# Down projection of a gated MLP: 36 of 43 input tiles in seven block products for eight

## The chip, the cores and the metric

The kernel runs on one core of one Trainium2 chip. The metric is the device time of one execution in microseconds. Three runs of the kernel before took 2181.3, 2181.68 and 2183.76 us; their median is 2181.68 us. The core has TensorE (matmuls, PE in the rows; PEld is its weight load, which overlaps), VectorE (DVE), ScalarE (ACT), GpSimd (POOL) and SyncE (SP). In this kernel SP issues nearly all loads and POOL the writes to memory and the accumulating loads.

## The reference, cut to what matters

One layer of a hybrid block on 512 tokens of width 2048 with a prefix of 256 context tokens. What the change touches is the gated MLP at the end:

```python
FFN_DIM = ((8 * D_MODEL // 3 + 127) // 128) * 128      # 5504 = 43 tiles of 128

def conv_ffn(h, w_up, cw, cb, w_down):
    u = dwconv3(h @ w_up, cw, cb)
    a, g = jnp.split(u, 2, axis=-1)
    return (a * jax.nn.silu(g)) @ w_down

mod_l = (jax.nn.silu(c) @ w_ada[l] + b_ada[l])[:, None, :]
sh_a, sc_a, gt_a, sh_f, sc_f, gt_f = jnp.split(mod_l, 6, axis=-1)
...
hf_l = modulate(rms_norm(x, g_ffn_norm[l]), sh_f, sc_f)
x = x + gt_f * conv_ffn(hf_l, w_up[l], ffn_conv_w[l], ffn_conv_b[l], w_down[l])
return rms_norm(x, g_final)
```

All data are float32. The gate `gt_f` (the last 16 of the 96 column tiles of `w_ada`) is needed only where the down projection ends.

## The kernel before

Activations lie transposed: a tile is 128 features by 512 tokens. Every float32 operand of a large product is split into a rounded part and the rest (`hilo`, `split`, `split4`: a cast on ScalarE, then a subtraction on VectorE), and `mm3` (L170 to L174) makes three matmuls of it: high by high, high by low, low by high. `late_both` works off the column tiles of `w_ada` beside other work: each tile is 1 MB, in two halves, and each half is one VectorE product-and-sum of 128 x 1024 (L240). Column tiles 32 to 79 are done before the up projection and 80 to 95 in the first group of the down projection.

The out projection (`whole`, L889) makes one output tile of 128 features at a time from one row of weights, in four splits of 512 columns. Its last two output tiles are made in two halves of the tokens, so that the norm after it can begin.

The up projection (loop over `f`, from L1129) makes one input tile of the down projection per turn, its gate and its value together. It takes input tiles, tokens and these two outputs in pairs, and makes seven block products of 256 columns (`product`) in place of eight. Two of the weight sums come from loads that add into a tile already loaded (`up_load`, issued by POOL), two from VectorE (L1144, L1145). Two of the seven products of a tile (`finish`) are made in the next turn. `acts` does convolution, gate and product, and writes the tile to memory (`y_d`, L990).

The down projection walks over three groups of output tiles, `DG` = 6, 6 and 4, one PSUM bank per output tile. Within a group it goes through all 43 input tiles: a load of weights, a load of the tile `y`, a split of both, and `n` times `mm3` on 512 columns. Loads are issued three input tiles ahead. In the last group the last eight input tiles are held on chip and done for the first half of the tokens, then for the second, so that the final norm of the first half runs beside the second. `down_end` (L1193) multiplies by the gate and adds the residual.

The order of the instructions on each engine is made by a planner, which works through the program by priority and by its own costs; each engine then works in that order. `keep` holds chosen instructions in the order of the program. Background generators (`bg`, advanced by `pump`) put small steps between products. The ring `t2` has 58 buffers of 128 x 512. In the up projection 56 of them hold its operands.

Of the kernel before, what the change touches and what calls it, by code (L numbers as in the profile page):

```python
# [17 lines left out]
P = 128  # L18
# [22 lines left out]
DG = [(0, 6), (6, 6), (12, 4)]  # L41

LAST = 8
# [3 lines left out]
NORM_AT = [(0, 3), (0, 7), (1, 7)]  # L47
# [15 lines left out]
def block_kernel(ctx, tc, xt, ctxt, ctxn, c, c_ctx, w_ada, small, w_in, w_inc, w_q, w_kv, w_out,  # L63
                 w_out_first, w_up, w_up_first, w_dn0, w_dn1, w_dn2, consts, out):
# [17 lines left out]
    y_d = dr.tile([NF, P, T], F32, name="y_d")  # L82
# [150 lines left out]
    late = {"t": 32, "raw": None, "end": 80}  # L233
# [655 lines left out]
    def whole(raw, xs, nm, ps=None, cols=slice(0, T), ld=None):  # L889
# [55 lines left out]
    for m in range(NK - 2):  # L945
        x_tile(m)
        residual(m, pss[m] if m < G else whole([load(w_out[m - G], D, f"o{m}r")], mix, f"o{m}", ld=ada_spare))
# [5 lines left out]
    for h in range(2):  # L953
        for i in range(2):
            residual(NK - 2 + i, whole(raws[i], mix, f"o{NK - 2 + i}{h}", pso[i], HS[h]), HS[h])
# [4 lines left out]
    assert late["t"] == 80 and late["raw"] is None  # L960
    SP.dma_start(sv_d, sv)
    ph1.close()
    rw = ctx.enter_context(tc.tile_pool(name="rw", bufs=1, side="right", reuse_waits="tile"))
    cp = ctx.enter_context(tc.tile_pool(name="cp", bufs=1, side="right", reuse_waits="tile"))
# [19 lines left out]
    def acts(f, g, a):  # L984
# [5 lines left out]
        G_.dma_start(y_d[f], ua)  # L990
# [122 lines left out]
    down_order = deque((g, k) for g in range(len(DG)) for k in range(NF))  # L1113

    def down_fetch():
        if down_order:
            g, k = down_order.popleft()
            raw = raw4(f"d{g}{k}")
            SP.dma_start(raw[:, :DG[g][1] * P], (w_dn0, w_dn1, w_dn2)[g][k])
            y = tmp([P, T], F32, f"y{g}{k}")  # L1120
            SP.dma_start(y, y_d[k])
            fetched.append((g, k, raw, y))

    def down_ahead():
        for _ in range(AHEAD):
            down_fetch()
# [4 lines left out]
    for f in range(G // 2, NF):  # L1131
# [3 lines left out]
        else:  # L1135
            down_ahead()
# [25 lines left out]
    for i in range(2):  # L1162
        svs[i] = raw4(f"sv2{i}")
        SP.dma_start(svs[i], sv_d[:, i * 1024:(i + 1) * 1024])

    def ada_late(t):
        r = []
        for i in range(2):
            r.append(raw4(f"adl{t}{i}"))
            SP.dma_start(r[i], w_ada[t][:, i * 1024:(i + 1) * 1024])  # L1170
        return r

    def down_operands(held=False):

        g, k, raw, y = fetched.popleft()
        down_fetch()
        n = DG[g][1] * P
        if held:
            w = hilo(raw[:, :n], n, f"dw{g}{k}")
        else:  # L1180
            w = split4(raw[:, :n], n, f"dw{g}{k}")
        return w, hilo(y, T, f"yh{g}{k}")
# [3 lines left out]
    def x_load(ms):  # L1186
        for m in ms:
            xl[m] = t2([P, T], F32, f"xl{m}")
            SP.dma_start(xl[m], x_d[m])

    def down_end(m, ps, cols=slice(0, T)):
        x = xl[m][:, cols]
        return V.scalar_tensor_tensor(out=x, in0=ps[:, cols], scalar=mod[:, 80 + m:81 + m], in1=x, op0=ALU.mult, op1=ALU.add)  # L1193
# [10 lines left out]
    def scale_out(j, h):  # L1204
        o = t2([P, 2, T // 2], F32, f"out{j}{h}")
        for i in range(2):
            A.activation(o[:, i], xl[j + i][:, HS[h]], AF.Identity, scale=s("g_fin", j + i))
        return o

    ssq = t2([P, T], F32, "eq")  # L1210
    todo = []
    late["end"] = 96
    late_load(ada_late)
    for g, (m0, n) in enumerate(DG):
        ps = [bank8(f"d{g}{i}") for i in range(n)]
        tail = LAST if g == len(DG) - 1 else 0
        for k in range(NF - tail):
            w, y = down_operands()
            for i in range(n):
                mm3(ps[i], part(w, i), y, k == 0, k == NF - 1 - tail)  # L1220
            if g == 0 and k % 2:
                late_both(ada_late)
            if k == NF // 2:
                x_load(range(m0, m0 + n))
            if todo and k > 2:
                m = todo.pop(0)
                if m:
                    add_squares(ssq, xl[m], T, f"eq{m}")
                else:
                    A.activation(ssq, xl[0], AF.Square)  # L1230
        if not tail:
            for i in range(n):
                down_end(m0 + i, ps[i])
            todo = list(range(m0, m0 + n))
            continue
        last = [down_operands(held=True) for _ in range(tail)]
        outs = []
        for h in range(2):
            sqs = [ssq]
            for i in range(n):  # L1240
                for q, (w, y) in enumerate(last):
# [121 lines left out]
```

## Time and profile before

| | |
|---|---|
| three runs, median | 2181.68 us |
| profiled execution | 2188.47 us, its span 2186.6 us |
| TensorE granted clock, mean | 0.994 |
| TensorE busy | 2144.9 us, 98% of the span, 13258 matmuls |
| VectorE, ScalarE, GpSimd busy | 1594.5, 1010.9, 112.9 us |
| DMA | 466.75 MB, mean 213 GB/s |

The busy time of TensorE is a sum of modelled spans that overlap, so a stage's cost is better read from the start of its first matmul to the start of the next stage's. Idle time of an engine that nothing waits for costs nothing. DMA share is the mean busy share of the 16 DMA engines.

### The profile page before, as it was taken

Reading aid. Unit: us, or ns where it says so; the run is one execution under the profiler, and the core shown is the slowest. Engines: PE = TensorE matmul, PEld = TensorE weight load, DVE = VectorE, ACT = ScalarE, POOL = GpSimd, SP = SyncE. Lnnn points to the kernel's source line nnn. Section 1 sums busy time; section 2 is a strip of 40 time slices with the busy share of each in tenths; the row PEclk is TensorE's granted clock in tenths of the full one; section 3 lists DMA queues with packets and bytes.
Section 4 is the critical chain, followed back from the end, with each engine's and each line's share of the span. In section 5 each row is a group of like instructions: output and inputs, shape, how many; then the busy total and the mean of one; then the engine's idle time right before and its main releaser. Section 6 shows DMA issues by size and latency. Waiting matters only on the chain.

```text
span 2186.6 us, 34349 instructions
## 1 busy us (share of the span) xinstructions
PE 2144.9 (98%) x13258; PEld 1913.1 (87%) x13258; DVE 1594.5 (73%) x2462; ACT 1010.9 (46%) x1636; POOL 112.9 (5%) x149
## 2 busy tenths in 40 slices
PE   7999999999999999999999999999999999999998
PEld 4788788888878888999999999999999888888887
DVE  7998987688896868877777777777776873632544
ACT  5533333655542246555555545555554432532444
POOL 0000000000000000101111110111110000000000
PEclk9999999999999999999999999999999999999999
DMA  9979885434469945677777777777776994752562
GB/s 337 334 275 333 275 278 163 140 121 166 158 244 354 326 164 136 162 203 204 189 195 197 203 188 198 202 191 196 197 200 201 362 336 151 254 160 90 170 202 87
DMA packets 144697, 466.75 MB, mean 213 GB/s; under 512 B 16338, under 2 KB 20690, under 8 KB 138898
## 3 DMA queue, kind: packets, MB, share of 16 engines
q1 hardware_dynamic: 126084, 405.03, 54.5%
q0 software_dynamic: 16272, 57.42, 12.9%
q8 instruction: 104, 1.70, 0.3%
q10 hardware_dynamic: 2176, 2.10, 0.3%
q14 instruction: 61, 0.50, 0.1%
HBM read 442.73 MB, written 20.71 MB: 212 GB/s over the span
## 4 chain that ended last, share of the span: by engine, by line
PE 94%; DVE 3%; DMA 2%; ACT 1%; issue 0%; SPq 0%; DVEq 0%; ACTq 0%
PE d L172 7%; PE d L173 7%; PE d L174 7%; PE pp L172 4%; PE pp L174 4%; PE pp L173 4%; PE o L172 1%; PE o L173 1%; PE o L174 1%; PE of L172 1%; PE of L173 1%; PE of L174 1%; PE uf L172 1%; PE uf L174 1%; PE uf L173 1%; PE pf L173 1%
## 5 line engine op out<-in xcount | busy, mean ns | idle before, releaser
L155 ACT CAST w_0h<-rw 128x512 fp32r<-128x512 f32 (+1 forms) x63 | 38.4, 618 | 110.4 <-PE pp L173 64.7
L1048 POOL DMA_DIRECT2D u_s<-in_w_up x80 | 68.0, 850 | 405.7 <-DMA u_s<-in_w_up 341.7
L218 DVE SCALAR_TENSOR_TENSOR ada<-ada,sv 128x1024 f32<-128x1024 f32 x64 | 78.0, 1226 | 4.3 <-DMA ada<-in_w_ada 4.0
L499 DVE SCALAR_TENSOR_TENSOR ada<-ada,svc 128x1024 f32<-128x1024 f32 x64 | 76.0, 1223 | 1.9 <-DMA ada<-in_w_ada 1.9
L240 DVE SCALAR_TENSOR_TENSOR ada<-ada,sv 128x1024 f32<-128x1024 f32 x52 | 62.7, 1222 | 7.1 <-DMA ada<-in_w_ada 7.1
L156 DVE TENSOR_TENSOR w_0l<-rw,w_0h 128x512 fp32r<-128x512 f32 (+1 forms) x63 | 43.0, 688 | 22.5 <-ACT w_0h L155 20.4
L240 DVE SCALAR_TENSOR_TENSOR ra<-ra,sv 128x1024 f32<-128x1024 f32 x44 | 52.6, 1222 | 1.1 <-DMA ra<-in_w_ada 1.0
L1145 DVE TENSOR_TENSOR u<-u,u 128x1024 f32<-128x1024 f32 x40 | 49.0, 1225 | 1.2
L1144 DVE TENSOR_TENSOR u<-u,u_s 128x1024 f32<-128x1024 f32 x40 | 48.8, 1220 | 0.4 <-DMA u_s<-in_w_up 0.3
L990 POOL DMA_DIRECT2D y_d<-a x43 | 24.7, 575 | 397.1 <-DVE a L989 387.3
L762 POOL TENSOR_TENSOR gr<-gr,half 128x8 f32<-128x8 f32 x4 | 10.1, 2522 | 630.1 <-DVE gr L761 537.6
L733 ACT CAST pth<-t 128x384 fp32r<-128x384 f32 x64 | 28.6, 485 | 26.4 <-PE t L730 26.4
L240 DVE SCALAR_TENSOR_TENSOR adl<-adl,sv 128x1024 f32<-128x1024 f32 x32 | 38.8, 1220 | 0.7 <-DMA adl<-in_w_ada 0.7
L510 DVE TENSOR_TENSOR acc<-acc,pp 128x512 f32<-128x512 f32 x50 | 34.5, 690 | 1.9 <-PE pp L174 1.9
L734 DVE TENSOR_TENSOR ptl<-t,pth 128x384 fp32r<-128x384 f32 x64 | 33.3, 553 | 2.6 <-ACT pth L733 2.6
L714 DVE TENSOR_REDUCE mn<-s 128x1 f32<-128x768 f32 x32 | 30.5, 955 | 4.8 <-PE s L703 4.6
L979 ACT ACTIVATE g<-cg,sm 128x512 f32<-128x512 f32 x40 | 32.5, 812 | 0.0
L979 ACT ACTIVATE a<-ca,sm 128x512 f32<-128x512 f32 x40 | 32.1, 803 | 0.0
L987 ACT ACTIVATE g<-g 128x512 f32<-128x512 f32 x43 | 27.2, 634 | 7.4 <-DVE g L981 7.4
L717 ACT ACTIVATE p<-s,mn 128x768 f32<-128x768 f32 x32 | 29.3, 916 | 1.6 <-DVE mn L714 1.3
L981 DVE SCALAR_TENSOR_TENSOR g<-cg,sm,g 128x511 f32<-128x511 f32 x40 | 29.9, 746 | 0.0
L980 DVE SCALAR_TENSOR_TENSOR a<-ca,sm,a 128x511 f32<-128x511 f32 x40 | 29.8, 746 | 0.0
(15581 smaller groups left out, 8733.5 us busy)
## 6 DMA issues: line engine op xcount, KB each, us to landing
ada<-in_w_ada SPq DMA_DIRECT2D x180, 512.0 KB, 5.7
u<-in_w_up SPq DMA_DIRECT2D x120, 512.0 KB, 8.1
u_s<-in_w_up SPq DMA_DIRECT2D x80, 512.0 KB, 4.0
u_s<-in_w_up POOLq DMA_DIRECT2D x80, 512.0 KB, 9.2
d<-in_w_dn SPq DMA_DIRECT2D x86, 384.0 KB, 3.9
y<-y_d SPq DMA_DIRECT2D x129, 256.0 KB, 4.5
ra<-in_w_ada SPq DMA_DIRECT2D x22, 1024.0 KB, 4.8
adl<-in_w_ada SPq DMA_DIRECT2D x32, 512.0 KB, 6.1
```

Of the source, the lines that this page charges most:

```text
L155: A.copy(out=hi[:, :n], in_=raw[:, a:a + n])
L156: V.tensor_tensor(out=lo[:, :n], in0=raw[:, a:a + n], in1=hi[:, :n].bitcast(F32), op=ALU.subtract)
L172: PE.matmul(ps, w[0], x[0], start=first, stop=False, skip_group_check=on_top)
L173: PE.matmul(ps, w[0], x[1], start=False, stop=False, skip_group_check=on_top)
L174: PE.matmul(ps, w[1], x[0], start=False, stop=last, skip_group_check=on_top)
L218: V.scalar_tensor_tensor(out=r, in0=r, scalar=1.0, in1=vec[:, i * 1024:(i + 1) * 1024], op0=ALU.mult, op1=ALU.mult, accum_out=col[:, i:i + 1])
L240: keep(V.scalar_tensor_tensor(out=r, in0=r, scalar=1.0, in1=svs[i], op0=ALU.mult, op1=ALU.mult, accum_out=lc[:, t % 4:t % 4 + 1] if i else ...
L499: keep(V.scalar_tensor_tensor(out=raw[q], in0=raw[q], scalar=1.0, in1=svc[:, q * 1024:(q + 1) * 1024], op0=ALU.mult, op1=ALU.mult, accum_o ...
L979: A.activation(u, src, AF.Identity, bias=s("fb", m), scale=s("fw", 86 + m))
L1048: G_.dma_start(r[-1], src[more], accum_op=ALU.add)
L1144: V.tensor_tensor(out=a11, in0=a11, in1=s1, op=ALU.add)
L1145: V.tensor_tensor(out=a12, in0=a12, in1=a11, op=ALU.add)
```

## The change

Nothing before the end of the out projection changes but the pace of `w_ada`: column tiles 80 to 87 are now worked off in the out projection too (`late["end"]` 88; a third `late_both` per output tile from tile 10 on, and some in the last two tiles). Tiles 88 to 95 follow beside the down projection in quarters (`gate_mods`).

The first seven input tiles of the down projection (`STD`) are split in the up projection and written to memory as two parts. The other 36 form 18 pairs. For each pair the seven operands of the block products, 128 x 256 in two parts side by side, are made beside the up projection (`pair_sums`) and written to memory (`t_d`), one of the seven after each product.

The down projection first does the seven tiles as before, on 512 columns and with eight PSUM banks, in two halves of the output (`h`), and copies the sums into 16 tiles `acc2`. Meanwhile it loads the operands of the first six pairs, the window: 42 tiles. Then come 24 steps. A step makes two output tiles from the six pairs of its window by seven products of six pairs each. Two of the seven are made in the next step. Each product is added to `acc2` by VectorE as it ends (`into`). From step to step the window either stays or slides by one pair, and then each product's oldest operand is replaced by a load right after the product. Steps 0 to 7 go over the 16 output tiles once while the window slides by five pairs; steps 8 to 15 and 16 to 23 do it again from the window six pairs on, so that each output tile gets its 18 pairs in three parts. The weights of a step are four blocks of 128 x 768; two sums come from VectorE, and one from VectorE after a load that adds. The gate is applied in the steps from 8 on. The last two steps are interleaved so that the first half of the tokens ends early.

```diff
-DG = [(0, 6), (6, 6), (12, 4)]
-LAST = 8
+STD = 7
+PAIRS = (NF - STD) // 2
+WIN = 6
+SLIDE = [0, 0, 1, 2, 3, 4, 5, 5]
+STEPS = 8 * PAIRS // WIN
+def window(st):
+    lo = SLIDE[st % 8] + st // 8 * WIN
+    return [(lo + j) % PAIRS for j in range(WIN)]
...
-            if a % 1024 == 0:
+            if a % 1024 == 0 or a == 512 and often:
                 late_both(ld)
...
-        G_.dma_start(y_d[f], ua)
+        if f < STD:
+            bg.append(plain(f, ua))
+        elif (f - STD) % 2 == 0:
+            even[0] = ua
+        else:
+            bg.append(pair_sums((f - STD) // 2, even[0], ua))
...
+    def pair_sums(p, e, o):
+        t = tmp([P, T], F32, f"ts{p}") if p == PAIRS - 1 else cp.tile([P, T], F32, tag="ts", bufs=1, name=f"ts{p}")
+        def put(n, src):
+            z = t2([P, T], F32R, f"tp{p}{n}")
+            A.copy(out=z[:, :256], in_=src)
+            V.tensor_tensor(out=z[:, 256:], in0=src, in1=z[:, :256].bitcast(F32), op=ALU.subtract)
+            G_.dma_start(t_d[p, OPS.index(n)], z.bitcast(F32))
+        put("11", e[:, H0])
+        yield
+        V.tensor_tensor(out=t[:, H0], in0=e[:, H0], in1=e[:, H1], op=ALU.subtract)
+        put("1", t[:, H0])
+        yield
...
@@ product of the up projection
             mm3(ps[:, :256], part(w, j), operand(n, j), first and j == 0, j == 7, on_top=not first)
+        pump(1)
...
+    for h in range(2):
+        ps = [bank8(f"d{h}{i}") for i in range(8)]
+        for k in range(STD):
+            plain_fetch()
+            if h == 0 and k + 2 < STD:
+                y_load(k + 2)
+            w = split4(fetched.popleft(), 1024, f"dw{h}{k}")
+            for i in range(8):
+                mm3(ps[i], part(w, i), y[k], k == 0, k == STD - 1)
+            pump(1)
+            for _ in range(2):
+                next(gm, None)
+            for _ in range(2 if h == 0 else 3):
+                win_load(*first.pop(0))
+        for i in range(8):
+            acc2.append(t2([P, T], F32, f"c{8 * h + i}"))
+            A.copy(out=acc2[-1], in_=ps[i])
...
+    def weights_of(st):
...
+        SP.dma_start(z.a11, src[0])
+        SP.dma_start(z.s1, src[2])
+        SP.dma_start(z.a12, src[1])
+        V.tensor_tensor(out=z.s3, in0=z.a11, in1=z.s1, op=ALU.add)
+        G_.dma_start(z.s1, src[3], accum_op=ALU.add)
+        SP.dma_start(z.a22, src[3])
+        return z
+    def seven(z, ps, a, n, nm, first):
+        hi = dw.tile([P, WIN * P], F32R, tag="wh", bufs=4, name=nm + "h")
+        lo = dw.tile([P, WIN * P], F32R, tag="wl", bufs=4, name=nm + "l")
+        A.copy(out=hi, in_=a)
+        V.tensor_tensor(out=lo, in0=a, in1=hi.bitcast(F32), op=ALU.subtract)
+        for j, p in enumerate(z.win):
+            x = win[n, p]
+            mm3(ps[:, :256], part((hi, lo), j), (x[:, :256], x[:, 256:]), first and j == 0, j == WIN - 1, on_top=not first)
+        if z.out is not None:
+            win_load(n, z.new)
+    def into(z, i, cols, ps, minus=False):
+        o = acc2[z.m + i][:, cols]
+        if z.st < 8:
+            V.tensor_tensor(out=o, in0=o, in1=ps[:, :256], op=ALU.subtract if minus else ALU.add)
+        else:
+            g = ng[:, z.m + i:z.m + i + 1] if minus else mod[:, 80 + z.m + i:81 + z.m + i]
+            V.scalar_tensor_tensor(out=o, in0=ps[:, :256], scalar=g, in1=o, op0=ALU.mult, op1=ALU.add)
+    def d_p2(z):
+        seven(z, z.pb, z.a12, "21", "p2", True)
+        into(z, 0, H0, z.pb)
+        V.tensor_tensor(out=z.a11, in0=z.a11, in1=z.s1, op=ALU.add)
+        V.tensor_tensor(out=z.a12, in0=z.a12, in1=z.a11, op=ALU.add)
...
+    def wt(nm):
+        return dw.tile([P, WIN * P], F32, tag="raw", bufs=12, name=nm)
...
+    for st in range(STEPS - 2):
+        z = nxt
+        nxt = weights_of(st + 1)
+        x_load(st + 1)
+        gate(st)
+        d_p1(z)
...
+        d_p2(z)
+        if prev is not None:
+            d_q4(prev)
+        d_p6(z)
+        d_q5(z)
+        next(gm, None)
...
+        if prev is not None:
+            d_q3(prev)
+            ended(prev)
+        d_p7(z)
+        prev = z
```

## Rows read from the trace of the kernel before

**Rows 1.** The page's engines: busy us, share of the span, instructions.
```profile
PE 2144.9 (98%) x13258; PEld 1913.1 (87%) x13258; DVE 1594.5 (73%) x2462; ACT 1010.9 (46%) x1636; POOL 112.9 (5%) x149
```

**Rows 2.** The chain that ended last: shares by engine; one piece (start, us, what).
```profile
PE 94%; DVE 3%; DMA 2%; ACT 1%; issue 0%; SPq 0%; DVEq 0%; ACTq 0%
...
1656.22 7.37 DMA d<-in_w_dn
```

**Rows 3.** Stretches: length; PE, PEld, DVE, ACT, POOL busy (instructions); clock, DMA share, GB/s.
```profile
730.00:775.00 45.00, 45.00 (x195) 36.52 (x194) 35.51 (x67) 12.37 (x20) 2.16 (x4) 1.00 0.90 315
775.00:812.00 37.00, 36.46 (x254) 33.79 (x253) 21.49 (x44) 16.81 (x30) 2.69 (x5) 1.00 0.28 89
1200.00:1400.00 200.00, 200.00 (x1669) 200.00 (x1668) 149.51 (x170) 104.09 (x140) 22.22 (x30) 1.00 0.74 197
...
1690.00:1730.00 40.00, 40.00 (x184) 32.76 (x184) 34.12 (x54) 19.74 (x30) 0.54 (x1) 1.00 0.92 329
```

**Rows 4.** What TensorE waited for: us in total, times, longest.
```profile
PE d L172 <- ACT dw00h L972: 0.8, 1, 0.8
...
PE u42b L174 <- DVE u42p2l L973: 0.4, 1, 0.4
```

**Rows 5.** TensorE in order of time: start, us, line, out<-in, shapes.
```profile
1230.45 0.28 PE L172 MATMUL u20a<-T20h,u20p6h 128*128 128x256 f32 x1
...
1233.33 0.28 PE L172 MATMUL u20c<-T10h,u20q5h 128*128 128x256 f32 x1
...
1684.29 0.50 PE L172 MATMUL d<-yh00h,dw00h 128*128 128x512 f32 x1 [0.80 <-ACT dw00h L972]
...
1866.55 0.39 PE L172 MATMUL d<-yh042h,dw042h 128*128 128x512 f32 x1
...
1870.75 0.39 PE L172 MATMUL d<-yh10h,dw10h 128*128 128x512 f32 x1
```

**Rows 6.** Groups of instructions (busy us, mean ns) and single lines (ns min/median/max).
```profile
L240 DVE SCALAR_TENSOR_TENSOR ada<-ada,sv 128x1024 f32<-128x1024 f32 x52 | 62.7, 1222 | 7.1 <-DMA ada<-in_w_ada 7.1
...
L1108 DVE TENSOR_TENSOR cg<-u5c,u x1: 425/425/425, 948.4 to 948.4; 128x256 f32<-128x256 f32 x1
...
L1100 ACT COPY u<-u10a x3: 365/365/367, 1021.2 to 1038.8; 128x256 f32<-128x256 f32 x3
...
L973 DVE TENSOR_TENSOR dw01l<-d,dw01h 128x768 fp32r<-128x768 f32 x1 | 1.0, 959 | 3.2 <-ACT dw01h L972 3.2
...
L972 ACT CAST dw07h<-d 128x768 fp32r<-128x768 f32 x1 | 0.8, 842 | 1.5 <-PE d L173 1.5
...
L932 DVE SCALAR_TENSOR_TENSOR x<-o,mod,x 128x512 f32<-128x512 f32 x8 | 6.0, 750 | 3.3 <-PE o L174 3.3
```

**Rows 7.** SP, POOL, VectorE and ScalarE in order of time around two tiles' weight loads.
```profile
1241.91 2.80 SPq L1046 DMA_DIRECT2D u_s<-in_w_up  x2
...
1246.26 0.86 POOL L1048 DMA_DIRECT2D u_s<-in_w_up  x1 [7.03 <-DMA u_s<-in_w_up]
...
1256.69 1.22 DVE L1144 TENSOR_TENSOR u<-u,u_s 128x1024 f32<-128x1024 f32 x1
...
1265.09 1.05 ACT L972 CAST u22p6h<-u 128x1024 fp32r<-128x1024 f32 x1 [1.56 <-PE u22b L173]
...
1662.33 0.62 ACT L306 CAST yh00h<-y 128x512 fp32r<-128x512 f32 x1 [4.24 <-DMA y<-y_d]
```

**Rows 8.** DMA: page's issues; 1200 to 1400: queues, accumulating loads; GB/s, 40 slices, 1698 to 1730.
```profile
ada<-in_w_ada SPq DMA_DIRECT2D x180, 512.0 KB, 5.7
...
q1 hardware_dynamic: 7181, 26.15, 40.1%
q0 software_dynamic: 3631, 12.91, 33.4%
...
u_s<-in_w_up POOLq DMA_DIRECT2D x20, 512.0 KB, 9.4
...
GB/s 282 271 376 279 211 330 311 284 325 277 187 236 241 278 278 302 341 398 401 415 410 412 435 417 392 385 403 389 398 399 403 402 392 402 405 393 407 387 402 401
```

More of the change, by code (lines that the diff above doesn't have):

```diff
@@ L1135, in block_kernel @@
         else:
-            down_ahead()
+            for _ in range(AHEAD):
+                plain_fetch()
         pa, pb, pc = (bank8(f"u{f}{z}") for z in "abc")
@@ L1184, in block_kernel @@
-    xl = {}
[L1186 to L1193, printed above, removed]
+    phc.close()
+    dp = ctx.enter_context(tc.tile_pool(name="dp", bufs=1, reuse_waits="tile"))
+    ssq = dp.tile([P, T], F32, name="ssq")
+    svq = []
+    for i in range(4):
+        svq.append(dp.tile([P, T], F32, name=f"svq{i}"))
+        SP.dma_start(svq[i], sv_d[:, i * T:(i + 1) * T])
@@ new lines, in block_kernel @@
+    drain()
+    class Step:
+        pass
+    def weights_of(st):
+        z = Step()
+        z.st, z.win, z.m = st, window(st), 2 * (st % 8)
+        nxt = window(st + 1) if st + 1 < STEPS else z.win
+        z.out, z.new = (None, None) if nxt == z.win else (z.win[0], nxt[-1])
+        n = WIN * P
+        src = [w_dnw[st][:, b * n:(b + 1) * n] for b in range(4)]
+        z.a11, z.s1, z.a12, z.s3, z.a22 = (wt(f"v{st}{x}") for x in ("11", "s1", "12", "s3", "22"))
+        SP.dma_start(z.a11, src[0])
[5 more added lines that the diff above has]
+        return z
@@ new lines, in d_q4, with d_q3, squares, ended @@
+    def d_q4(z):
+        seven(z, z.pa, z.a22, "4", "q4", False)
+        into(z, 1, H0, z.pa, True)
+    def d_q3(z):
+        seven(z, z.pc, z.a12, "22", "q3", False)
+        into(z, 0, H1, z.pc)
+    begun = []
+    def squares(m, cols=slice(0, T)):
+        x = acc2[m][:, cols]
+        if not begun:
+            begun.append(A.activation(ssq, x, AF.Square))
+        else:
+            add_squares(ssq, x, cols.stop - cols.start, f"eq{m}{cols.start}", a=cols.start)
+    def ended(z):
+        if z.st >= STEPS - 8:
+            for i in range(2):
+                squares(z.m + i)
@@ new lines, in block_kernel @@
+    za, zb = nxt, weights_of(STEPS - 1)
+    d_p1(za)
+    d_p2(za)
+    d_q4(prev)
+    d_p1(zb)
+    d_p2(zb)
+    d_p6(za)
+    d_q3(prev)
+    ended(prev)
+    d_p6(zb)
+    for z in (za, zb):
+        squares(z.m, H0)
+    d_p7(za)
+    d_p7(zb)
+    d_q4(za)
+    sqs = [ssq, add_squares(None, acc2[za.m + 1][:, H0], T // 2, "eqa", a=0)]
+    scaled = {j: scale_out(j, 0) for j in range(0, za.m, 2)}
+    d_q4(zb)
+    sqs.append(add_squares(None, acc2[zb.m + 1][:, H0], T // 2, "eqb", a=0))
+    bg.append(rms_steps(sqs, D, 0, T // 2, rl, wait=1, one=True))
@@ L1259, in block_kernel @@
+    outs = final(0, rl[:, HS[0]], scaled)
+    d_q5(za)
+    squares(za.m + 1, H1)
+    pump(2)
+    d_q5(zb)
+    squares(zb.m + 1, H1)
+    pump(1)
+    scaled = {j: scale_out(j, 1) for j in range(0, za.m, 2)}
+    for _ in range(3):
+        next(outs)
+    d_q3(za)
+    sqs = [ssq, add_squares(None, acc2[za.m][:, H1], T // 2, "eqc", a=T // 2)]
+    for _ in range(3):
+        next(outs)
+    d_q3(zb)
+    sqs.append(add_squares(None, acc2[zb.m][:, H1], T // 2, "eqd", a=T // 2))
     *_, r = rms_steps(sqs, D, T // 2, T // 2, None, one=True)
```

201 lines of the change are left out of this document (109 added, 92 removed).

## The prediction

> **What bounds the kernel now.** I read the engine totals first: TensorE is busy in 2144.9 of 2186.6 us [rows 1]. The reader is to see that no other engine comes near it. Then the chain that ended last: 94% of it is TensorE [rows 2], so the kernel is a queue of matmuls and a change is worth what it takes out of that queue, less the gaps that it opens. Then the stages: in both projections that the change touches TensorE is busy for the whole of a stretch at granted clock 1.00 [rows 3]. The list of TensorE's waits shows only two of note in them, 0.8 and 0.4 us, both where the up projection ends [rows 4]. So before and after differ by the number of matmuls, by what one costs, and by new gaps. "Within 0.2%" below means within 4.4 us, about what these runs can tell apart.
>
> **Price of a matmul.** 24 matmuls of 256 columns run from 1230.45 to 1233.33: 0.120 us each. 18 of 512 columns run from 1866.55 to 1870.75: 0.2333 us each [rows 5]. Two halves therefore cost 0.240 for 0.2333, 2.9% more: the change pays this on what it cuts up.
>
> **Matmuls removed.** Before: 43 input tiles x 16 output tiles x 3 passes = 2064 of full width, but the last eight input tiles of the last group (8 x 4 x 3 = 96) run as 192 halves. 1968 x 0.2333 + 192 x 0.120 = 482.2 us. Check: the first one starts at 1684.29, the group's 774 end at 1870.75, and 774 x 0.2333 plus the 48 matmuls of the last two up products (5.8) is 186.4 of these 186.5 us [rows 5]. After: 7 x 16 x 3 = 336 of full width (78.4 us), and 24 steps x 7 products x 6 pairs x 3 = 3024 of 256 columns (362.9 us; a step is 126 of them, 15.1 us). Sum 441.3. **Gain 40.9 us.** This needs every new matmul to find its operands; the rest is about that.
>
> **Out projection: eight more tiles of w_ada.** They move from the old down stage. Each brings two VectorE sums of 1.22 us [rows 6], so 16 sums, 19.5 us, and 8.4 MB. Four come with output tiles 10 to 13, whose weight splits run at about 730 to 775. There VectorE is busy 35.5 of 45 us and DMA has a share of 0.90 at 315 GB/s [rows 3]. With 8 x 1.22 more VectorE has 45.3 us of work in 45, and 4.2 MB lift DMA to 408 GB/s, against some 400 that a saturated stretch shows [rows 8]: both are just full. The other four come in the next 37 us, VectorE 21.5 busy, DMA 0.28 [rows 3]. Room there is ample, but the last rows of w_out hold two of the four buffers, so load and sums alternate: 4 x (5.7 [rows 8] + 2.4) = 32.6 us, which just ends before the up projection's first weights want the same memory. Bounds: 0, if all is hidden as the earlier ones are, to 9.8, if the first four tiles' sums all stand in front of splits. I take 3, near the low end, since the overshoot by these rows is about 1 us and the chain's lateness can add some.
>
> **Up projection: sums made beside it.** Per pair seven times a copy of 256 columns on ScalarE (0.365 us), a subtraction on VectorE (0.425), a write of 256 KB from POOL's queue, and three more VectorE operations of that width [rows 6]. Per tile of 20.16 us that is 3.5 x 0.425 + 1.5 x 0.425 = 2.1 us for VectorE, which goes from 15.1 (149.5 of 200 us [rows 3]) to 17.2, 85%, and 1.3 for ScalarE, from 10.5 to 11.8. TensorE never waited at 75%. What could: the copies go through the two spare buffers of that ring, and their write stands on POOL behind an accumulating load that waits some 4 us for its plain load [rows 7]. Bounds: 0 to 7.2 (one wait of 0.4 [rows 4] in each of 18 pairs). I take 0.5.
>
> **Up to down.** The wait of 0.8 [rows 4] comes where ScalarE stood 4.24 us for the first y before it could cast the up projection's weights [rows 7]. That cast is gone, since y now comes back already split: a gain of up to 1.2 us. Against it stands that the first y needs buffers that the up projection's operands still hold, as the first down weight once stood 7.4 us on the chain [rows 2]. Between -1.2 and +7.4 I take 0.
>
> **Seven tiles as before, and the first window.** In 78.4 us come 14 weight loads (7.3 MB), 14 halves of y (3.7), 35 window tiles (9.2), 28 quarters of w_ada and four of the vector (8.4), and the first step's weights (2.0): 30.6 MB, with the next step's weights and the last pair's seven writes 34.4. At 400 GB/s [rows 8] this is 77 to 86 us: DMA is full. Weights go three ahead (16.8 us) and y two ahead, so most of a delay is absorbed. Bounds 0 to 7.6 (86 less 78.4); I take 1.
> The Trainium skill ("DMA: Bandwidth & Descriptors", Where 436 GB/s comes from) says that transfers between HBM and SBUF are bound at about 358 GB/s a core. By that rule the 34.4 MB would take an estimated 96 us. The trace disagrees: 400 GB/s is held for some 18 us [rows 8], so the measurement decides.
>
> **Into the steps.** The first step needs the sum s1 + its fourth block, which passes a load, an addition, an accumulating load and a cast. Bounds 0 (loaded in time) to 14.0 (the chain of rival 3, 18.3, less two products, 4.3). I take 2, since the loads compete with the full DMA just described.
>
> **The steps themselves.** ScalarE per step: 7 casts x 0.84 = 5.9 of 15.1 us. VectorE: 7 splits and 3 sums x 0.96, 7 eliminations x 0.425 [rows 6] = 12.6; in steps 8 to 15 two gates of 0.75 more [rows 6], in the last eight two additions of squares, which I price alike: 14.1 of 15.1. So VectorE is full but not over. DMA: 4 x 0.393 plain + 0.393 accumulated, and in 17 of 24 steps seven window tiles, 1.835 MB. By the plain queue's rate in the up stage (26.15 MB in 40.1% of 200 us, 326 GB/s) and the accumulating queue's (12.91 MB in 33.4%, 193) [rows 8] a sliding step takes 10.5 + 2.0 = 12.5 us, with x loads 14.1. It fits, barely in eight. Bounds 0 to 9.6 (0.4 in each step); I take 1.
>
> **Tail.** After the last product come one elimination, a square, the root and eight outputs, as now. I take 0; another order of the last products can save or add about one of them, 2.2 us.
>
> **Sum.** -40.9 + 3 + 0.5 + 0 + 1 + 2 + 1 + 0 = -33.4. The profiled execution took 2188.5 (2186.6 and 1.9 around the span), 0.3% above the median of 2181.7, so the sum is made against 2188.5, giving 2155.1, and the same difference against the median gives **2148 us**. Range of this case alone: 2143 to 2160.
>
> **Rivals.**
> 1. Nothing waits: 2181.7 - 40.9 and a saved 1.2 at the seam, 2140 to 2143. For it: TensorE had no wait over 0.4 us through 40 tiles of the same scheme. Against it: VectorE goes from 75% to between 83 and 93% by durations, and it works in order.
> 2. The operands come late by DMA: the full 7.6 between the projections, 6.8 more at the out projection than I took, and about 1 in each of the eight barely fitting steps, in place of the 1 and 0 that I took. 2148 + 6.6 + 6.8 + 8 = 2169.4. For it: a saturated share of 0.92 between 1690 and 1730 [rows 3] on less traffic. Against it: TensorE was busy all through that stretch. The skill's 358 GB/s would put it here too.
> 3. Slower than before: the accumulated weight sets the pace of a step. Its chain, worked out from [rows 6 to 8]: 4.3 from issue to POOL, 0.96 for the third sum that must read s1 before, 0.85 issue, 9.4 to landing, 0.96 to add, 0.84 and 0.96 to cast and split: 18.3. If the memory for the next s1 comes free only when the fourth product of this step has read its own, six products (13.0 us) lie between, and each step stalls 5.3 us: 23 x 5.3 = 122, 2270 us. It decides from 33.4 / 23 = 1.5 us a step. For it: the step is 15.1 us where an up tile had 20.2. Against it: twelve buffers for five a step leave two beyond two full steps, and with nine for five the same load was issued at 1241.91, used at 1256.69 and needed at 1265.09 [rows 7], 8.4 us to spare.
>
> **Chances.** Forecast 0.56, nothing waits 0.17, late by DMA 0.15, slower 0.08, and 0.04 for delays of some 29 to 38 us that just eat the gain. So faster by over 0.2%: 0.88, within: 0.04, slower: 0.08. The range 2139 to 2172 takes in the forecast, rival 1 and rival 2.
>
> **What would show it.** Right: between the last up product and the last matmul some 445 us; the steps' matmuls 0.120 us apart; a step every 15.1 us at clock 1.00; few waits of TensorE there. Out projection: the first up matmul about 3 us later than now. Wrong: steps longer than 15.5 us with TensorE waiting for a cast whose releaser is the accumulating load (rival 3) or a window tile (rival 2); up tiles over 20.3 us; a lower granted clock in the steps.

## The result and the profile after

The changed kernel took 2162.36 us (median of four: 2154.39, 2160.57, 2164.15, 2164.22), the kernel before beside it 2182.72. The ratio is 0.9897, 95% interval 0.9882 to 0.9912. In a later group the same kernel took 2158.79 against 2185.69, ratio 0.9881 (0.9863 to 0.9900). It is faster by 20 to 27 us where 33 were forecast. All its runs lie in the range of 2139 to 2172, and none is as fast as the forecast of 2148. The first median lies outside the forecast's own range of 2143 to 2160, the second inside.

The profiled execution after is the fastest of its four: 2154.39 us, span 2152.4, granted clock 0.995. That of before, 2188.47 us, is slower than all four of its runs. So the traces are compared stage by stage, not by their ends.

The page's engines and the chain's shares, after (as in [rows 1, 2]):

```profile
PE 2092.9 (97%) x14458; PEld 1936.3 (90%) x14458; DVE 1770.2 (82%) x2859; ACT 1047.3 (49%) x1709; POOL 188.6 (9%) x270
...
PE 88%; DMA 5%; DVE 4%; issue 1%; ACT 1%; SPq 0%; POOL 0%; DVEq 0%; ACTq 0%; POOLq 0%
```

TensorE is busy for 52 us less. But its share of the chain fell from 94% to 88%, and DMA's rose from 2 to 5: the chain now passes transfers in the out projection, in the up projection and on the way into the steps. Which of them cost time, TensorE's waits tell (as in [rows 4]); its single waits over 1 us from the end of the out projection on:

```profile
PE v0a L181 <- ACT v0p6h L1304: 6.5, 1, 6.5
...
PE rs L298 <- DVE fq0t L333: 3.3, 1, 3.3
...
PE rs L298 <- ACT eqdt L329: 2.2, 1, 2.2
...
PE v0a L181 <- ACT v0p1h L1304: 1.4, 1, 1.4
...
PE v22a L183 <- DVE v22p7l L1305: 1.2, 1, 1.2
```

and the one of the kernel before at the end of the out projection:

```profile
PE rs L289 <- DVE fq0t L324: 1.7, 1, 1.7
```

In these names `v0` is the first step and `v0p1h`, `v0p1l` are the rounded part and the rest (the low half) of the weights of its product p1; `v0s` stands for its s1 and its s3, `v` for its other blocks, `c` for `acc2`, `aq` for the gate's quarters of `w_ada`, `fq` and `eq` for squares.

All of them stand where two stages meet: the first step (`v0`), the end of the out projection (`rs <- fq0t`) and the end of the program (`eqdt`, `v22`). The middles of the stages show no gap. Stretches of the up projection, the seven tiles, the way into the steps and the steps (as in [rows 3]):

```profile
1200.00:1400.00 200.00, 199.95 (x1677) 199.74 (x1676) 166.83 (x226) 115.27 (x175) 36.91 (x55) 1.00 0.80 229
...
1690.00:1765.00 75.00, 73.55 (x317) 59.18 (x315) 41.87 (x95) 24.36 (x37) 3.23 (x6) 1.00 0.94 339
...
1765.00:1780.00 15.00, 8.05 (x50) 7.61 (x51) 9.44 (x13) 3.22 (x5) 1.75 (x2) 0.81 1.02 331
...
1900.00:1960.00 60.00, 60.00 (x508) 60.00 (x507) 49.48 (x70) 23.42 (x28) 3.42 (x4) 1.00 0.82 238
```

In the steps TensorE is busy for 60.00 of 60 us, VectorE for 82%. In the third line it is busy for 8 of 15 us, and the granted clock falls to 0.81. How the gap there is made, first by ScalarE and VectorE in order of time:

```profile
1758.20 5.47 ACT L1276 COPY c<-d 128x512 f32<-128x512 f32 x8 [11.04 <-PE d L183]
1763.57 0.83 ACT L1304 CAST v0p1h<-v 128x768 fp32r<-128x768 f32 x1
```
```profile
1764.44 0.96 DVE L1305 TENSOR_TENSOR v0p1l<-v,v0p1h 128x768 fp32r<-128x768 f32 x1 [1.52 <-ACT v0p1h L1304]
1765.31 0.95 DVE L1294 TENSOR_TENSOR v0s<-v,v0s 128x768 f32<-128x768 f32 x1
```

and from there by the chain that ended last (start, us, what):

```profile
1761.31 5.46 DMA v<-in_w_dnw
1766.82 7.53 DMA v0s<-in_w_dnw
...
1774.37 0.97 DVE v L1329
...
1775.36 0.84 ACT v0p6h L1304
...
1776.25 0.58 PE v0a L181
```

ScalarE copies the last eight sums of the seven tiles and only then casts the first step's weights. VectorE works in order: the first low half, then s3 (L1294). The accumulating load must not write s1 before s3 has read it. It is issued 0.56 us after s3's end, and so it is in all eight traces that have this load; the profile names other releasers for it (here the load of a22, which landed just then). It takes 7.53 us, and an addition and a cast follow: 12.7 us from `v0p1h` to the third product, and TensorE has two products (4.3 us) to lay beside it. After that wait 18 matmuls run at 0.21 us, at a granted clock of 0.50, which is the level of 1.2 GHz.

The end of the program, VectorE in order of time:

```profile
2134.08 0.48 DVE L1319 SCALAR_TENSOR_TENSOR c<-v22c,mod,c 128x256 f32<-128x256 f32 x1 [0.54 <-PE v22c L183]
2134.70 3.70 DVE L1386 TENSOR_TENSOR out<-out,rl 128x512 f32<-128x512 f32 x6
2138.32 0.48 DVE L1319 SCALAR_TENSOR_TENSOR c<-v23c,mod,c 128x256 f32<-128x256 f32 x1
```

Six outputs of the first half stand between the last two eliminations (an elimination is VectorE's addition of a finished product to `acc2`). From the last product's last matmul (2136.12) to the end are 16.3 us, against 12.8 before, where the outputs of the first half began earlier:

```profile
2168.89 3.10 DVE L1200 TENSOR_TENSOR out<-out,rl 128x512 f32<-128x512 f32 x5 [0.25 <-ACT rl L296]
...
2173.79 0.28 PE L174 MATMUL d<-yh242h,dw242l 128*128 128x256 f32 x1
```

### The profile page after: what moved, and what is told of

Same layout as the page of the kernel before. It is cut to its first block, busy times and chain, and to the rows that moved or that the text cites. A ratio compares the mean times of both kernels' runs of the same rounds, so it can differ in the third digit from the quotient of the medians.

```text
span 2152.4 us, 37747 instructions
## 1 busy us (share of the span) xinstructions
PE 2092.9 (97%) x14458; PEld 1936.3 (90%) x14458; DVE 1770.2 (82%) x2859; ACT 1047.3 (49%) x1709; POOL 188.6 (9%) x270
## 4 chain that ended last, share of the span: by engine, by line
PE 88%; DMA 5%; DVE 4%; issue 1%; ACT 1%; SPq 0%; POOL 0%; DVEq 0%; ACTq 0%; POOLq 0%
PE pp L181 4%; PE pp L183 4%; PE pp L182 4%; PE o L181 1%; PE o L183 1%; PE o L182 1%; DMA ada<-in_w_ada 1%; PE uf L181 1%; PE uf L182 1%; PE uf L183 1%; PE of L181 1%; PE of L182 1%; PE of L183 1%; PE pf L182 1%; PE pf L183 1%
## 5 line engine op out<-in xcount | busy, mean ns | idle before, releaser
L1029 POOL DMA_DIRECT2D t_d<-tp x126 | 72.7, 580 | 461.6 <-DVE tp L1028 458.7
L249 DVE SCALAR_TENSOR_TENSOR ada<-ada,sv 128x1024 f32<-128x1024 f32 x68 | 82.0, 1218 | 13.1 <-DMA ada<-in_w_ada 13.1
L227 DVE SCALAR_TENSOR_TENSOR ada<-ada,sv 128x1024 f32<-128x1024 f32 x64 | 77.4, 1217 | 3.8 <-DMA ada<-in_w_ada 3.6
L1027 ACT CAST tp<-a 128x256 fp32r<-128x256 f32 x90 | 34.8, 406 | 66.5 <-DMA t_d<-tp 58.0
L165 DVE TENSOR_TENSOR w_0l<-rw,w_0h 128x512 fp32r<-128x512 f32 (+1 forms) x63 | 42.5, 680 | 21.8 <-ACT w_0h L164 21.6
L1028 DVE TENSOR_TENSOR tp<-a,tp 128x256 fp32r<-128x256 f32 x90 | 36.1, 417 | 13.5 <-ACT tp L1027 13.3
L1027 ACT CAST tp<-ts 128x256 fp32r<-128x256 f32 x36 | 14.6, 407 | 44.0 <-DMA t_d<-tp 42.2
L1028 DVE TENSOR_TENSOR tp<-ts,tp 128x256 fp32r<-128x256 f32 x36 | 15.1, 421 | 25.2 <-ACT tp L1027 25.2
L1233 DVE SCALAR_TENSOR_TENSOR aq<-aq,svq 128x512 f32<-128x512 f32 x32 | 21.1, 688 | 12.6 <-DMA aq<-in_w_ada 11.2
```

Of the source, the lines that this page charges most:

```text
L227: V.scalar_tensor_tensor(out=r, in0=r, scalar=1.0, in1=vec[:, i * 1024:(i + 1) * 1024], op0=ALU.mult, op1=ALU.mult, accum_out=col[:, i:i + 1])
L249: keep(V.scalar_tensor_tensor(out=r, in0=r, scalar=1.0, in1=svs[i], op0=ALU.mult, op1=ALU.mult, accum_out=lc[:, t % 4:t % 4 + 1] if i else ...
L1027: A.copy(out=z[:, :256], in_=src)
L1028: V.tensor_tensor(out=z[:, 256:], in0=src, in1=z[:, :256].bitcast(F32), op=ALU.subtract)
L1029: G_.dma_start(t_d[p, OPS.index(n)], z.bitcast(F32))
```

## The experiments

They ran in three groups, each beside the kernel before (2185.69, 2185.92 and 2185.19 us there). Since runs of one kernel spread over 4 to 17 us, the stages of their traces say more than the medians. This table is worked out from the starts of first matmuls: **A** from the first out projection tile to the first up product; **B** the first 216 matmuls of the steps (12 products, 25.6 us at 0.1187 us each); **C** the 2394 after them, as many as 19 steps have; **D** from the last product's last matmul to the end of the span. E1 is the changed kernel again. B ends where the third step's first product begins, but not in e10 to e12: there the planner begins that product one product earlier, after 198 matmuls (36.6, 28.7 and 29.1 us).

| | median us | ratio (95%) | A | B | C | D |
|---|---|---|---|---|---|---|
| before | 2182.72 | | 115.5 | | | 12.8 |
| changed | 2162.36 | 0.9897 (0.9882 to 0.9912) | 118.6 | 35.5 | 284.1 | 16.3 |
| e1 changed again | 2158.79 | 0.9881 (0.9863 to 0.9900) | 118.9 | 35.1 | 284.1 | 16.3 |
| e2 gate later | 2162.43 | 0.9895 (0.9880 to 0.9910) | 118.3 | 36.1 | 284.1 | 15.1 |
| e3 gate earlier | 2159.65 | 0.9879 (0.9865 to 0.9892) | 117.6 | 35.0 | 287.3 | 15.7 |
| e4 tail | 2157.79 | 0.9871 (0.9857 to 0.9884) | 118.1 | 35.7 | 284.1 | 16.3 |
| e5 first sum on VectorE | 2158.06 | 0.9872 (0.9858 to 0.9887) | 117.7 | 31.5 | 284.1 | 16.1 |
| e6 no late tiles | 2156.20 | 0.9861 (0.9848 to 0.9873) | 115.6 | 36.0 | 287.3 | 15.6 |
| e7 ten buffers | 2157.75 | 0.9874 (0.9861 to 0.9886) | 118.2 | 35.9 | 284.1 | 15.2 |
| e8 both seams | 2164.10 | 0.9907 (0.9888 to 0.9925) | 128.6 | 32.3 | 284.1 | 15.1 |
| e9 all sums on VectorE | 2160.94 | 0.9886 (0.9872 to 0.9899) | 117.4 | 31.0 | 291.0 | 15.2 |
| e10 gate in order | 2164.28 | 0.9893 (0.9875 to 0.9912) | 120.2 | 38.7 | 286.7 | 15.6 |
| e11 best | 2154.22 | 0.9856 (0.9842 to 0.9871) | 115.5 | 30.8 | 287.3 | 15.3 |
| e12 best, POOL | 2154.58 | 0.9858 (0.9843 to 0.9872) | 115.6 | 31.2 | 287.7 | 16.5 |

A lies between 117.4 and 120.2, and D between 15.1 and 16.3, in kernels that have these stages unaltered; so smaller differences than that say nothing by themselves.

**e1, the changed kernel again.**

> The changed kernel once more, unaltered, as the base of this group of runs. Theory (cold stretches and the spacing of TensorE's matmuls make the runs differ, the work does not): its runs lie between 2154 and 2165 us as the first four did, ratio to the kernel before 0.988 to 0.992; its trace shows again the wait of TensorE for the first step's accumulated weights (6 to 7 us) and a stretch at 1.2 GHz behind it, since nothing in the program's order has changed. Rival (the 6.5 us wait was an accident of one execution): that wait is below 3 us here and the time stays the same or falls.

The wait for the first step's sum was 5.1 us, with two stretches of 3.4 us at 1.2 GHz around it. It belongs to the program, though it is shorter than the 6 to 7 us expected. One of the five runs, 2168.3, lies above the 2154 to 2165 expected.

**e2 and e3, when the gate loads are issued.**

```diff
 e2, in the seven tiles
-            for _ in range(2):
+            for _ in range(1):
                 next(gm, None)
 ... and in each step
-        next(gm, None)
+        for _ in range(3):
+            next(gm, None)
 e3, in the seven tiles
-            for _ in range(2):
+            for _ in range(4 if h == 0 else 0):
                 next(gm, None)
```

> One load of gate modulation weights per input tile in the seven-tile stage instead of two, and three per step instead of one: 14 fewer transfers of 256 KB ahead of the first step's weights on SP's queue. Theory 1 (the first step is late because twelve of those loads, issued 1742.8 to 1756.2 us one ring buffer at a time, stand ahead of its weights in SP's order): the weights are issued some 10 us earlier, the wait of 6.5 us falls below 2 us, the stretch at 1.2 GHz behind it goes, and the time falls by 8 to 11 us against the unaltered changed kernel (to some 2150 us). Theory 2 (the transfers themselves fill the 16 DMA engines, which carry 339 GB/s there): 3.7 MB less in the stage is also some 10 us of transfers, so the wait falls likewise; this run tells neither from the other, the next one does. Rival 3 (the wait is the accumulation's own length): the wait stays above 5 us and the time moves by less than 2 us.

> Four loads of gate modulation weights per input tile in the first half of the seven-tile stage and none in the second: the stage moves as many bytes as in the changed kernel, but none of those loads stands just ahead of the first step's weights. Theory 1 (SP's order): the first step's wait falls below 2 us as in the run with later loads, total 8 to 11 us below the unaltered changed kernel, unless the first half now waits for its own weights (then less, 3 to 8 us). Theory 2 (the DMA engines are full in this stage whatever the order): the wait moves to the first half or to the first window's sums, and the total moves by less than 3 us.

The wait stayed: 4.9 and 4.8 us. But neither edit did what it said. SP's queue in e2, and in e3, in order of time:

```profile
1743.96 20.51 SPq L1231 DMA_DIRECT2D aq<-in_w_ada  x17
1764.56 0.38 SPq L1291 DMA_DIRECT2D v<-in_w_dnw  x1
```
```profile
1746.90 11.58 SPq L1231 DMA_DIRECT2D aq<-in_w_ada  x10
1758.53 0.42 SPq L1291 DMA_DIRECT2D v<-in_w_dnw  x1
```

The planner issued 17 and 10 of the loads in one run ahead of the first step's weights (12 in the changed kernel), wherever the program had put them. In e3 the first half also waited 1.1 us for its own weights. So theory 1 was not tried here; e10 tries it.

**e4, the outputs ahead of the last elimination.**

```diff
     sqs = [ssq, add_squares(None, acc2[za.m][:, H1], T // 2, "eqc", a=T // 2)]
-    for _ in range(3):
-        next(outs)
     d_q3(zb)
```

> The changed kernel without the three early steps of the first half's outputs ahead of the last elimination (they come after it). Theory (six output products of 3.7 us on VectorE stand ahead of the last elimination's subtraction, which was ready some 2 us earlier; the end of the program came 16.2 us after the last matmul against 12.8 us before): the tail shortens by 1.5 to 3 us. Rival (those outputs only move behind and end the program instead): the tail is as long or up to 2 us longer.

The wait for the last square fell from 2.2 to 0.4 us, and D stayed at 16.3: the three products came behind the root instead (five there in 3.08 us, where the changed kernel has two in 1.27). VectorE's last product ended 10.3 us after the last matmul, against 10.7. The rival holds. VectorE has some 16 products of 0.61 us to make after the first half's norm, in whichever order.

**e5, the first step's sum on VectorE.**

```diff
+        if st == 0:
+            SP.dma_start(z.a22, src[3])
+            V.tensor_tensor(out=z.s1, in0=z.s1, in1=z.a22, op=ALU.add)
+        else:
             G_.dma_start(z.s1, src[3], accum_op=ALU.add)
             SP.dma_start(z.a22, src[3])
```

> The changed kernel with one alteration: the first step's s1 + a22 is made by VectorE from the two loaded tiles, instead of by an accumulating load; all other steps keep the accumulating load. Theory 3 (the wait ahead of the first step's third product is a chain of latencies: the last eight evictions end, weights split, s3 made, then 7.5 us of accumulating load, then two additions and a split; TensorE has only the 36 matmuls of two products, 4.3 us, to lay beside it): a22 lands near 1768 us of the span, the addition takes 0.95 us, so TensorE waits 0 to 2 us instead of 5 to 6.5, part of the stretch at 1.2 GHz behind it goes too, and the time falls by 5 to 9 us against the unaltered changed kernel (to 2150 to 2154 us). Rival (the DMA engines are full there, so the first steps' weights and window tiles land late whichever way the sum is made): the wait moves to the landing of a22 or of the next step's weights, and the time falls by less than 2 us.

TensorE's waits on the way into the steps, in e5:

```profile
PE v0a L181 <- ACT v0p6h L1308: 1.5, 1, 1.5
PE v0a L181 <- ACT v0p1h L1308: 1.4, 1, 1.4
PE v1a L181 <- ACT v1p1h L1308: 1.0, 1, 1.0
```

The wait fell from 6.5 to 1.5 as theory 3 says, and B from 35.5 to 31.5. The gain of 4 us in B is under the 5 to 9 expected: a wait of 1.0 for the second step's weights came up behind it, and a stretch of 3.4 us at 1.2 GHz stayed. The medians (0.9872 against 0.9881) can't show 4 us; they moved by less than 2, as the rival had it.

**e6, without the eight late tiles.**

```diff
-    late = {"t": 32, "raw": None, "end": 88}
+    late = {"t": 32, "raw": None, "end": 80}
 ... no `often`, no `ld` in the last two tiles
+    V.tensor_copy(out=mod[:, 80:88], in_=s("b_ada", 80, 8))
```

> The changed kernel without the eight modulation tiles that the change adds to the out projection: columns 80 to 87 of the modulation take only their bias, so 8 MB of loads and 16 dots on VectorE are left out there. Theory (those dots stand ahead of the last residuals on VectorE and cost some 3 us at the seam to the up projection, 118.3 us from the first out projection tile to the first up product against 115.5 before): that stretch comes back to 115 to 116 us and the time falls by 2.5 to 4.5 us. Rival (the longer seam is the changed memory layout of the up projection, whose first tiles are released otherwise): the stretch stays above 117.5 us and the time moves by less than 1 us.

The kernel leaves out the product of these columns, so it measures and is no version. A came back to 115.6 and the wait at the norm to 1.7. So the eight tiles cost 3 us there, shown.

**e7, ten weight buffers.**

```diff
-        return dw.tile([P, WIN * P], F32, tag="raw", bufs=12, name=nm)
+        return dw.tile([P, WIN * P], F32, tag="raw", bufs=10, name=nm)
```

> The changed kernel with ten buffers for the steps' weights instead of twelve, that is two steps of five with nothing to spare. It asks how much of the accumulating load's length the steps hide. My reading (in the steady steps TensorE never waits, period 14.95 us; the accumulating load takes some 8 us and begins a step ahead): with ten buffers a step's first loads wait until the last product of the step before the previous one is split, so the sums come later; TensorE begins to wait, 0 to 3 us in each of 24 steps, total 0 to +40 us with +10 as the likeliest. Rival (the lead is far larger than needed): no wait, within 2 us of the unaltered changed kernel.

No wait between 1795 and 2100 us, and C the same. The likeliest that I had named, +10 us, was wrong and its rival right: the steps hide the accumulating load even with nothing to spare.

**e8, both seams.**

```diff
 (the edit of e5, and)
-    ... often=m > 9))
+    ... often=m > 5))
```

> The changed kernel with the first step's sum on VectorE, as in the run before last but two of this group, and the second modulation load per output tile begun four output tiles earlier (from the seventh instead of the eleventh), so that the last modulation tile is finished some output tiles before the last residuals. Theory: both seams shrink, 7 us for the first step and 2 to 3 us at the end of the out projection: 2148 to 2152 us. Rival (the second edit only moves the pressure of the loads on VectorE and the DMA engines to an earlier place): the same time as with the first edit alone.

Neither expectation came true: the second edit cost 10 us. TensorE's longest wait in the out projection, and SP's queue, in e8:

```profile
PE ol L181 <- ACT o150w0h L164: 10.5, 1, 10.5
```
```profile
759.70 32.19 SPq L143 DMA_DIRECT2D ada<-in_w_ada  x18
794.63 1.81 SPq L143 DMA_DIRECT2D o15r<-in_w_out  x2
```

18 modulation loads, which wait for the ring's buffers one by one, stand on SP ahead of the last output tile's weights, which use the same ring. Those were issued only at 794.6, and TensorE stood for 10.5 us.

**e9, every sum on VectorE.**

```diff
-        G_.dma_start(z.s1, src[3], accum_op=ALU.add)
         SP.dma_start(z.a22, src[3])
+        V.tensor_tensor(out=z.s1, in0=z.s1, in1=z.a22, op=ALU.add)
```

> The changed kernel with s1 + a22 made by VectorE in every step, from the tile of a22 that is loaded anyway, and no accumulating load at all. It asks from the other side what the accumulating load costs. My reading: VectorE is busy 82 to 87% of a step and gains 0.95 us in 14.95 (some 6%), so it still does not set the pace; TensorE does not wait in the steady steps, the period stays 14.95 or 15.12 us (its two observed values), the DMA engines carry 23 x 0.38 MB less, and the total is that of the run with the first step alone: from the first step's first product to the third step's first 31 to 32 us instead of 35 to 36. Rival (VectorE at 93% becomes late in some products): waits of TensorE for VectorE's low halves appear, period above 15.2 us, 5 to 15 us slower than with the first step alone.

B is 31.0 as in e5, but C grew by 6.9 us. Its waits in the early steps:

```profile
PE v4a L181 <- DVE c L1316: 2.0, 1, 2.0
...
PE v6a L181 <- DVE c L1316: 0.9, 1, 0.9
PE v7a L181 <- DVE c L1316: 0.5, 1, 0.5
```

They are for VectorE's eliminations, which free the sums' banks, and not for low halves as the rival named it. From the first step's first matmul to the last one the trace has 374.0 us, against 367.6 in e5 and 371.7 in the changed kernel. My reading was wrong and the rival holds in effect: the accumulating load spares VectorE what it has no room for in the early steps. The medians of e9 and e5 are not apart.

**e10, the gate loads held in order.**

```diff
+                with tc.issue_after(held[0]) if held[0] is not None else ExitStack():
                     SP.dma_start(r, w_ada[88 + i][:, q * T:(q + 1) * T])
 ... held[0] is the load of a22; one load per tile, three per step
```

> The changed kernel with the gate modulation loads held in the order of the queue: one per tile in the seven-tile stage, and three per step, each after the weights of the step that is already being loaded, so that 9 of them stand right ahead of the first step's weights on SP instead of 12 to 17 and 15 stand behind. The earlier two runs on this did not put them there: the planner moved the loads back ahead. Theory 1 (SP's order makes the first step late): its weights are issued 5 us or more ahead of where they were relative to its first product, TensorE's wait falls below 3 us. Theory 3 (the chain from the last evictions through s3 and the accumulating load does): the weights land earlier and nothing comes of it, since the splits wait for ScalarE's eight evictions: the wait stays at 4 to 6.5 us, and from the first step's first product to the third step's first it remains 35 to 36 us.

SP's queue, VectorE and TensorE's longest wait there, in e10:

```profile
1743.89 0.33 SPq L1294 DMA_DIRECT2D v<-in_w_dnw  x1
1744.50 0.33 SPq L1295 DMA_DIRECT2D v0s<-in_w_dnw  x1
```
```profile
1770.23 0.96 DVE L1308 TENSOR_TENSOR v0p1l<-v,v0p1h 128x768 fp32r<-128x768 f32 x1 [16.02 <-ACT v0p1h L1307]
1771.11 0.95 DVE L1297 TENSOR_TENSOR v0s<-v,v0s 128x768 f32<-128x768 f32 x1
...
1782.91 0.96 DVE L1332 TENSOR_TENSOR v<-v,v0s 128x768 f32<-128x768 f32 x1 [6.91 <-DMA v0s<-in_w_dnw]
```
```profile
PE v0a L181 <- ACT v0p6h L1307: 9.2, 1, 9.2
```

This settles it. a11 and s1 were asked for 26 us before the first product, where the changed kernel has 8, and s1 had landed 20.5 us before s3 began, where the changed kernel has 2.0. VectorE stood idle for 16 us and did not make s3, since in its order the first low half comes first, and that waits for ScalarE's eight copies. Beside the later loads the accumulating load took 10.3 us instead of 7.5, so the wait grew to 9.2 and B to 38.7 (36.6 up to the third step's first product), over the 4 to 6.5 and 35 to 36 that theory 3 named. Theory 1 falls; theory 3 stands in its order of causes. The loads put off into the steps cost 2.6 us in C, where TensorE waits for eliminations in four of the early steps. Putting s3 ahead of the low half on VectorE was not tried.

**e11 and e12, a better version.**

```diff
 (the edits of e5 and e10, five loads per step, and)
-    late = {"t": 32, "raw": None, "end": 88}
+    late = {"t": 32, "raw": None, "end": 84}
-    ... often=m > 9))
+    ... often=m > 11))
 ... gate_mods takes tiles 84 to 95
 e12, in `final`:
-            ins = V.tensor_tensor(out=o, in0=o, in1=rr, op=ALU.mult)
+            ins = (G_ if h == 0 and j in (2, 8) else V).tensor_tensor(out=o, in0=o, in1=rr, op=ALU.mult)
```

> First step's sum on VectorE, the gate loads behind the weights as in the run before, and four of the eight added modulation tiles taken out of the out projection (its last tile is 84 there, 12 tiles instead of 8 are dotted in quarters beside the down projection). Theory: 31 to 32 us from the first step's first product to the third step's first (35.5 in the changed kernel), and 116 to 117 us from the first out projection tile to the first up product (118.3): 4 us and 1.5 to 2 us, so 5 to 6 us below the changed kernel, ratio to the kernel before 0.985 to 0.987. Rival (the four tiles more beside the down projection, 4 MB and 16 x 0.7 us of VectorE in the steps, come back as waits there): no better than with the first step alone (0.987 to 0.988).

> The run before, and two of the first half's eight output products made by POOL instead of VectorE in the tail, where VectorE has 16 of them to make after the first half's norm (0.61 us each) and POOL is idle. Theory (VectorE's products are the tail): the tail from the last product's last matmul to the end shortens by 1 to 2 us (15.1 to 16.3 us in the changed kernel). Rival (POOL's own products are so long, or slow VectorE's so much, that they end last): the tail is as long or longer.

e11 is the fastest version by the median: 2154.22 us, 5 to 8 below the changed kernel, though its interval (0.9842 to 0.9871) still touches those of e1, e4, e5 and e7. Most of its gain is in A, 115.5. In the steps it does not beat e5: B is 30.8, 0.7 less, so the early weights bring next to nothing, and C gives 3.2 us back, 2.2 of it waits in the early steps where the added dots fill VectorE, as the rival has it, and 1.0 the longer spacing of the last section. From the first step's first matmul to the last one e11 takes 370.2 us, e5 367.6. e5's edit with the four tiles moved and no loads held was not tried. The stretch just after the seam in e11:

```profile
1800.00:1820.00 20.00, 19.46 (x162) 19.08 (x161) 19.82 (x39) 7.95 (x10) 1.69 (x2) 1.00 1.05 376
```

e12 gained nothing: D went from 15.3 to 16.5, and VectorE's last product ended 11.7 us after the last matmul instead of 10.5. POOL's two products and VectorE's in that stretch of e12:

```profile
L1392 DVE TENSOR_TENSOR out<-out,rl x4: 677/1219/1777, 2130.7 to 2134.7; 128x512 f32<-128x512 f32 x4
...
L1392 POOL TENSOR_TENSOR out<-out,rl x2: 1707/1747/1787, 2130.8 to 2132.5; 128x512 f32<-128x512 f32 x2
```

Beside POOL, VectorE's four took 4.66 us, where in e11 it made all six in 3.70; the two that began beside one of POOL's took 1.77 and 1.74 us, the other two 0.69 and 0.67. The Trainium skill ("SBUF — State Buffer", SBUF: two separate sides) says that a GpSimd instruction that reads SBUF and a VectorE instruction with two SBUF inputs hold one port pair by turns, and that whichever starts second stands still until the other has ended. These durations agree.

## Why the prediction was right, and which terms were mis-sized

The number came out right with some luck. 2162.36 is nearer to rival 2's 2169.4 than to the forecast's 2148, and only the traces tell the two apart: delays came at seams, by order and by length of chains, and not by late window tiles. The wide range took in the terms that were mis-sized, and a shorter spacing of matmuls that no term held hid part of them.

- **Matmuls, -40.9.** Right. 336 + 3024 ran as counted. A step took 14.95 us in most runs and 15.12 in others (15.1 forecast). In the trace shown the step's matmuls cost 0.1187 us each, not 0.120, which is 4 us more gain; see the last section.
- **Out projection, +3.** Measured +3.1 by the trace and 3 by e6. VectorE's dots run until 808.7, ahead of the last residual; the forecast's sum of loads and dots from 775 on came to 807.6.
- **Up projection, +0.5.** No wait. A tile took 20.16 us in both kernels, and 19.94 from some point on in most traces (see the last section). VectorE is at 83% (85 forecast). ScalarE waits 65 times, 100.1 us in all, for the two spare buffers' writes; VectorE waits 29 times, 38.5 us, for ScalarE's copies, and TensorE never.
- **Up to down, 0.** 1.0 us against 0.8 before.
- **Seven tiles, +1.** No wait within the stage, though DMA was full: a share of 0.94 over 75 us, and 397 GB/s from 1700 to 1720.
- **Into the steps, +2: the term that was mis-sized most.** It measured 11.5 us: 1.6 from the last plain matmul to the first step's first, and B less its matmuls, 35.5 - 25.6 = 9.9. The chain was in the text, with its bound of 14.0. I took 2 since I thought of it as a race of loads. e10 shows that earlier loads don't help: the sum can't be begun before ScalarE has emptied the eight banks, because s3 stands behind `v0p1l` on VectorE. In the changed kernel itself s1 landed at 1763.35 and s3 began at 1765.31, so with the loads where they are this order costs at most 2 us; the rest is the chain's length. The wait also brings a stretch at 1.2 GHz, which no term held.
- **The steps, +1.** Nothing: rival 3's chain is hidden, even with ten buffers (e7). VectorE was 82 to 87% busy.
- **Tail, 0.** It measured +2.3 to +3.5 (D), and 1.2 for a low half that VectorE made late. In the new scheme the first half of the tokens is final only after five of a step's seven products, so its norm and its outputs come when only four products are left; VectorE then has 16 products to make. It began them 4.90 us ahead of the last matmul in the kernel before and 1.42 us ahead in the changed one, 3.5 us later; no run here moved that start, so this cause is read from the traces and not tried. I had looked at what comes after the last product, not at what had been done by then.

So -40.9 + 3.1 + 11.5 + 3.5 + 1.2 is -21.6 at 0.120 us a matmul, and -25.6 with the steps at the shorter spacing. The medians gave -20.4 and -26.9. The two traces shown differ by 34.2, since 5.1 of that lies ahead of the out projection (698.6 us before, 693.5 after) and some 4 in the shorter spacing of the up projection's second half. The forecast's -33.4 lacks the 9.5 of the way in and the tail's 4.7. Rival 1 (nothing waits) was true of every stage's middle and of the seam between the projections, and of no other seam. Rival 2 fails: no wait of TensorE ends on a window tile. Its sum is also 1 us too long: the forecast had taken 1 for the steps, not 0. Rival 3's chain came true once, at the first step, not 23 times.

## What to carry to other kernels

Where a stage's first operands pass through a chain (load, sum, accumulating load, sum, cast), price the way in as that whole chain less the work that lies beside it, begun where its first engine comes free; a full pipeline hides it in every later step, and the first one pays for it. An accumulating load is worth it where VectorE is the tighter engine, and it can be left out for the first step alone (e5, e9). Before judging an edit to the order of loads, look at the queue in the trace: the planner may have put it back. And count the work between two marks before comparing the time between them, since a planner can move a product across a mark.

## What the runs showed of the hardware

- **One program, two matmul spacings.** With TensorE busy throughout and the clock at 1.00, an up tile took 20.16 us in some stretches and 19.94 in others, and a step 15.12 or 14.95 (0.1200 or 0.1187 us a matmul). In the trace of the changed kernel it changed near 1280 us, in the middle of a stage, without a wait. In e3 the steps ran at the long spacing throughout; in e6 the up projection went over to the short one near 1600 us and the steps ran at the long one again, and e11 went back to the long one from about 1820 to 1900 us. Over 36 up tiles and 24 steps this is up to 8 and 4 us, as much as the edits tried here. What sets it stays open.
- **A wait costs more than its length.** Where TensorE waited for 4.8 to 9.2 us at the first step, the granted clock stood at 0.50, that is 1.2 GHz, for 6.8 to 10.2 us around it. At the end of the out projection, with a wait of some 3 us, it did so for 3.4 to 10.2 us. With 1.6 or 1.7 us there it did not in before, e6, e8 and e12, but it did in e11 (6.8 us).
